# Four instead of three of eight K-tile pairs by seven products in the gate and up phases of a two-layer encoder trunk

## The chip, the core and the metric

One Trainium2 chip; the kernel runs on one of its cores. The metric is the device time of one execution in microseconds (us). TensorE (PE) does the matrix products, with its weight loads (PEld) beside them; VectorE (DVE) and ScalarE (ACT) do the elementwise work; GpSimd (POOL) does next to nothing here; SyncE (SP) issues the loads of weights.

## What is computed

Two layers over x (256 rows, 2048 columns, float32): layer 0 is an attention and convolution mixer, layer 1 a gMLP mixer with a layer norm, and each is followed by an RMSNorm and a SwiGLU block of hidden width 5632. The change lies in the SwiGLU blocks above all:

```
def swiglu(h, w_gate, w_up, w_down):
    return (jax.nn.silu(h @ w_gate) * (h @ w_up)) @ w_down

for layer in range(2):
    h = rms_norm(x, mix_norm[layer])
    x = x + (mixer_ab(h, ...) if layer == 0 else mixer_c(h, ...))
    h = rms_norm(x, ffn_norm[layer])
    x = x + swiglu(h, w_gate[layer], w_up[layer], w_down[layer])
return rms_norm(x, final_norm)
```

## The kernel before

**Precision.** Every large product is float32 by three matmuls (`three`, L439): each operand is split into a high part in fp32r (a cast on ACT) and a low part (source minus high part, a subtraction on DVE), and high x high, high x low and low x high are added up in PSUM. For weights the tiles are `raw` (as loaded), `whi` and `wlo`.

**Phases and steps.** The phases are ab_in, ab_out, up0, down0, c_in, c_out, up1, down1. A phase is cut into blocks of 512 output columns, a block into steps. A step takes 4 tiles of weights of 128x512: in an ordinary phase four K-tiles; in up0 and up1 a pair of K-tiles of the gate and the same pair of the up matrix. `whi` and `wlo` have two buffers each and `raw` has three, so the parts of step t+1 are made while PE works on step t, into the buffers that step t-1 has left.

**Up phases** (`run_mixed`, L501). Eleven blocks of eight steps, steps 0 to 7 of a block here. A step is a 2x2x2 product of blocks (two row halves, two K-tiles, gate and up), done in one of two ways, as the string `MIX` says: kind N by eight products, kind S by seven (Strassen's way). Each product is three matmuls of 128x512, so an N step has 24 and an S step 21. All products of a block go into seven accumulators q1 to q7, one PSUM bank each (`BANKS`, L490); the bank left over takes transposes. N uses the raw weight tiles. S needs sums of them in `tt` (`combine_first` L203, one subtraction of 128x1024; `combine_rest` L212, two of 128x512), `whi` and `wlo` of `tt`, and for three products also high and low parts `ha`, `la` of three raw tiles (`prep_a` L196, 128x1536). `tt`, `ha` and `la` have one buffer each. The activations come in matching sums, their parts are `fh` and `fl` (`x_forms`, L377).

**End of a block** (`ends`, L830). Seven additions on DVE with one ACT copy turn the accumulators into gate `sg` and up `hh` (`first`, `sums_a`, `sums_b`), ACT applies Silu (`gate`), DVE multiplies (`product`, two instructions). `h_transposes` (L819) then turns `hh` by two groups of four transposes on PE, each followed by an ACT copy to `h`. In an up phase both groups use the one spare bank, so the second group waits for the first copy, and the second copy for the second group.

**Order.** ACT and DVE run what the code emits in the order in which it emits it (`manual_schedule`), in the up phases throughout; PE's order is set by a scheduler when the program is built. At the end of step t the code emits the preparation of step t+2 (`prep`, L220): in an up phase both casts, then the jobs listed for `before[t+1]`, then the low part in two instructions of 128x1024. `end_step` does the same in the ordinary phases. Jobs put off by `later` are emitted at their due half step (`jobs_due`).

Of the kernel before, what the change touches and what calls it, by code (L numbers as in the profile page):

```python
# [16 lines left out]
P = 128  # L17
S = 256
# [28 lines left out]

MIX = "NNSNSNSN"  # L50

# [9 lines left out]
def trunk_kernel(  # L61
# [134 lines left out]
    def prep_a(t):  # L196

        hi = mixw[0].tile([P, 3, NB], F32R, tag="ha", name="ha")
        lo = mixw[0].tile([P, 3, NB], F32R, tag="la", name="la")
        split(hi, lo, raws[t][:, 1:4, :])  # L200
        parts_a[t] = (hi, lo)

    def combine_first(t):  # L203

        load(t)
# [6 lines left out]
    def combine_rest(t):  # L212

        r, tt = raws[t], sums[t]
# [5 lines left out]
    def prep(t, between=()):  # L220

        if t >= len(steps) or t in parts:
            return
        load(t)
        s = steps[t]
        r = sums.pop(t) if s.kind == "S" else raws[t]
        hi = wpool.tile([P, RC, NB], F32R, tag="whi", name="whi", bufs=W_BUFS)
        lo = wpool.tile([P, RC, NB], F32R, tag="wlo", name="wlo", bufs=W_BUFS)
        halves = [slice(0, 2), slice(2, 4)]
        if s.kind == "std":  # L230
            for fn in between:
                fn()
            for h in halves:
                split(hi[:, h, :], lo[:, h, :], r[:, h, :])
        else:
            for h in halves:
                nc.scalar.copy(hi[:, h, :], r[:, h, :])  # L237
            for fn in between:
                fn()
            for h in halves:  # L240
                nc.vector.tensor_tensor(  # L241
                    out=lo[:, h, :], in0=r[:, h, :], in1=hi[:, h, :].bitcast(F32),
                    op=ALU.subtract,
                )
        parts[t] = (hi, lo)
        if s.pi in operand:
            operand[s.pi].split(s.k0 // RC)

    sums = {}
    operand = {}  # L250

# [249 lines left out]
    def run_mixed(pi, lhs, ends):  # L501

        mixed[0] = True
        order = ExitStack()
        order.enter_context(  # L510
            tc.manual_schedule(engines={mybir.EngineType.Activation, mybir.EngineType.DVE})
        )
# [5 lines left out]
        last_s = MIX.rindex("S")  # L518
        ps, seen, left = {}, set(), {}
        before = {t: [] for t in range(lo_t, hi_t + 3)}  # L520
        after = {t: [] for t in range(lo_t - 1, hi_t + 3)}
        for t in range(lo_t, hi_t):
            i = (t - lo_t) % n
            if steps[t].kind != "S":
                continue
            early = i == MIX.index("S") and t - 3 >= lo_t
            (after[t - 3] if early else before[t - 2]).append(lambda t=t: combine_first(t))
            after[t - 2].append(lambda t=t: combine_rest(t))
            after[t - 1].append(lambda t=t: prep_a(t))
        for t in range(lo_t + n - 1, hi_t, n):  # L530
            first, sums_a, sums_b, gate, product = ends(steps[t].key, ps)
            after[t - n + 1 + last_s].append(first)
            after[t].insert(0, sums_a)
            before[t + 1][0:0] = [sums_b, gate]
            before[t + 2].insert(0, product)
        for fn in before[lo_t]:
            fn()
        for t in range(lo_t, hi_t):
# [9 lines left out]
            prods = LAST_S if i == last_s else PRODUCTS[s.kind]  # L548
            for j, (q, fa, group, slot) in enumerate(prods):
# [10 lines left out]
            for fn in after[t]:  # L560
                fn()
            parts_a.pop(t, None)
            del parts[t]
            cur[0] += 1
            load(t + LOAD_AHEAD)
            if t + 1 < hi_t:
                prep(t + PREP_AHEAD, before[t + 1])
            else:
                order.close()
                prep(t + PREP_AHEAD)  # L570
                for fn in before[t + 1] + before[t + 2]:
                    fn()
        mixed[0] = False

    cur = [0]
# [238 lines left out]
    def ffn(pi, st, nst):  # L814
# [14 lines left out]

        def ends(j, ps):  # L830


            def first():
                g = fpool.tile([P, M, NB], F32, tag="sg", name="sg")
                h = fpool.tile([P, M, NB], F32, tag="hh", name="hh")
                left[j], right[j] = g, h
# [4 lines left out]
            def sums_a():  # L841
                g, h = left[j], right[j]
                add(h[:, 0, :], ps[2], h[:, 0, :])
                add(g[:, 0, :], ps[5], g[:, 0, :])
                add(g[:, 1, :], ps[5], h[:, 1, :])

            def sums_b():
                g, h = left[j], right[j]
                add(g[:, 0, :], ps[3], g[:, 0, :])
                add(h[:, 1, :], ps[4], h[:, 1, :])  # L850

            def gate():
                g = left[j]
                for m in reversed(range(M)):
                    nc.scalar.activation(
                        g[:, m, :], g[:, m, :], AF.Silu, scale=st.r[:, m : m + 1]
                    )

            def product():
                g, h = left.pop(j), right.pop(j)  # L860
# [7 lines left out]
            return first, sums_a, sums_b, gate, product  # L868

        run_mixed(pi, st, ends)  # L870
        close_pool("forms", "mixw")
        xpool[0] = open_pool("x_next", "left")
        hT.split_pool = open_pool("split", "left")
        operand[pi + 1] = hT
        for n in range(PREP_AHEAD):
            hT.split(n)
# [41 lines left out]
    def layer_norm():  # L918
# [20 lines left out]
        for n in range(4):  # L939
            sl = slice(n * NB, (n + 1) * NB)  # L940

            def block(sl=sl):
                for m in range(M):
                    a = vt[:, m, sl]
                    nc.vector.tensor_scalar(  # L945
                        out=a, in0=a, scalar1=mu[:, m : m + 1], scalar2=rs[:, m : m + 1],
                        op0=ALU.add, op1=ALU.mult,
                    )
                    nc.vector.tensor_tensor(out=a, in0=a, in1=lng[:, sl], op=ALU.mult)  # L949
                    nc.vector.tensor_tensor(out=a, in0=a, in1=lnb[:, sl], op=ALU.add)  # L950
# [156 lines left out]
```

## Time and profile before

| | |
|---|---|
| time, median of three runs | 2119.1 us (2117.6 to 2122.2) |
| the profiled execution: its time / its span | 2118.6 us / 2116.7 us |
| busy: PE, DVE, ACT | 99%, 71%, 53% of the span |
| granted PE clock, mean | 0.994 of full speed |
| up0 | from 390.3 to 861.9 us of the span |
| up1 | the same length, from 1390 us on |

Views used: the page's totals and its chain of waits; windows, which give the busy time of each engine in a stretch; and timelines of one engine, in which a row is a run of like instructions with its start, its length, and in brackets the idle time before it and what ended that. DVE and ACT begin an instruction before the one in front of it has ended, so what an instruction costs its engine is the distance from start to start. The same holds for PE.

### The profile page before, as it was taken

How to read it: one execution, taken by the hardware profiler on the slowest of the kernel's cores; microseconds unless marked ns; L12 is line 12 of the kernel's file. 1: busy time of each engine (PE TensorE's matmuls, PEld its weight loads, DVE VectorE, ACT ScalarE, POOL GpSimd, SP SyncE). 2: the span in 40 equal slices, each digit the busy share in tenths (PEclk: the TensorE clock that was granted, in tenths of full speed). 3: DMA queues.
4: the chain of work that ended last, by engine and by line, in shares of the span. 5: the costliest groups of instructions: out<-in, count | busy, mean ns of one | idle time of the engine just before them, and what ended most of it. 6: DMA issues, size and time to landing. Idle time of an engine off the chain costs nothing.

```text
span 2116.7 us, 24028 instructions
## 1 busy us (share of the span) xinstructions
PE 2086.0 (99%) x9356; PEld 1722.0 (81%) x9356; DVE 1504.7 (71%) x1597; ACT 1115.7 (53%) x1318; POOL 17.8 (1%) x37
## 2 busy tenths in 40 slices
PE   8999999999999999999999999999999999999998
PEld 6888888788888888788888878878888888878886
DVE  4545556788888888667664465578888888866675
ACT  5444445555555555555555534555555555555554
POOL 1000000000000000000000000000000000000000
PEclk9999999999999999999999999999999999999999
DMA  6555555465556555655555554546555655555554
GB/s 243 182 173 174 185 184 194 160 206 192 201 196 203 195 200 194 232 186 191 195 191 189 181 173 169 195 160 213 184 199 199 209 189 199 200 198 193 188 196 139
DMA packets 205345, 404.80 MB, mean 191 GB/s; under 512 B 9420, under 2 KB 10032, under 8 KB 204976
## 3 DMA queue, kind: packets, MB, share of 16 engines
q1 hardware_dynamic: 203296, 397.45, 55.4%
q0 software_dynamic: 1328, 4.77, 0.7%
q8 instruction: 73, 1.20, 0.2%
q10 hardware_dynamic: 608, 1.06, 0.1%
q14 instruction: 40, 0.33, 0.0%
HBM read 401.14 MB, written 2.10 MB: 191 GB/s over the span
## 4 chain that ended last, share of the span: by engine, by line
PE 95%; DVE 1%; DMA 1%; ACT 1%; issue 1%; SPq 0%; POOLq 0%; POOL 0%; ACTq 0%; DVEq 0%
PE b L440 31%; PE b L442 31%; PE b L441 31%; PE b L346 2%; DMA raw<-in_ab_w_in_dram 1%; DVE wlo L194 1%; ACT whi L193 0%; PE b L382 0%; PE b L961 0%; PE b L653 0%; ACT junk L929 0%; DVE vt L949 0%; DVE vt L945 0%; PE b L697 0%; ACT ha L193 0%
## 5 line engine op out<-in xcount | busy, mean ns | idle before, releaser
L194 DVE TENSOR_TENSOR wlo<-raw,whi 128x1024 fp32r<-128x1024 f32 x400 | 471.7, 1219 | 244.4 <-ACT whi L193 244.3
L193 ACT CAST whi<-raw 128x1024 fp32r<-128x1024 f32 x400 | 400.0, 1049 | 257.8 <-PE b L442 217.4
L441 PE MATMUL b<-wlo,fh 128*128 128x512 f32 x1144 | 448.9, 393 | 0.0
L442 PE MATMUL b<-whi,fl 128*128 128x512 f32 x1144 | 445.1, 389 | 0.0
L440 PE MATMUL b<-whi,fh 128*128 128x512 f32 x1144 | 381.1, 392 | 0.0
L237 ACT CAST whi<-raw 128x1024 fp32r<-128x1024 f32 x220 | 220.3, 1050 | 177.0 <-PE b L442 93.4
L241 DVE TENSOR_TENSOR wlo<-raw,whi 128x1024 fp32r<-128x1024 f32 x220 | 258.9, 1218 | 34.3 <-ACT whi L237 34.3
L441 PE MATMUL b<-wlo,jh 128*128 128x512 f32 x704 | 275.4, 391 | 0.4 <-DVE wlo L194 0.4
L442 PE MATMUL b<-whi,jl 128*128 128x512 f32 x704 | 274.6, 390 | 0.7 <-DVE jl L194 0.7
L440 PE MATMUL b<-whi,jh 128*128 128x512 f32 x704 | 250.4, 392 | 6.1 <-ACT jh L193 6.1
L441 PE MATMUL b<-wlo,xh 128*128 128x512 f32 x640 | 253.1, 396 | 1.9 <-DVE wlo L194 1.9
L442 PE MATMUL b<-whi,xl 128*128 128x512 f32 x640 | 251.6, 394 | 0.3 <-DVE xl L371 0.3
L440 PEld LDWEIGHTS b<-whi,fh 128*128 128x128 f32 x1144 | 213.6, 188 | 45.6 <-ACT whi L237 0.6
L442 PEld LDWEIGHTS b<-whi,fl 128*128 128x128 f32 x1144 | 215.0, 188 | 43.4
L441 PEld LDWEIGHTS b<-wlo,fh 128*128 128x128 f32 x1144 | 214.8, 188 | 43.3
L440 PE MATMUL b<-whi,xh 128*128 128x512 f32 x640 | 243.5, 399 | 2.6 <-ACT xh L367 2.6
L194 DVE TENSOR_TENSOR jl<-h,jh 128x1024 fp32r<-128x1024 f32 x88 | 107.6, 1224 | 152.9 <-ACT jh L193 152.9
L237 ACT CAST whi<-tt 128x1024 fp32r<-128x1024 f32 x132 | 134.7, 1053 | 128.7 <-PE b L442 90.3
L193 ACT CAST jh<-h 128x1024 fp32r<-128x1024 f32 x88 | 92.6, 1054 | 204.4 <-PE b L441 204.4
L241 DVE TENSOR_TENSOR wlo<-tt,whi 128x1024 fp32r<-128x1024 f32 x132 | 157.2, 1220 | 58.0 <-ACT whi L237 58.0
L440 PEld LDWEIGHTS b<-whi,jh 128*128 128x128 f32 x704 | 132.5, 189 | 34.0 <-ACT jh L193 6.9
L442 PEld LDWEIGHTS b<-whi,jl 128*128 128x128 f32 x704 | 132.7, 189 | 29.8 <-DVE jl L194 2.2
(148 smaller groups left out, 2308.3 us busy)
## 6 DMA issues: line engine op xcount, KB each, us to landing
raw<-in_ffn_w_gate_dram SPq DMA_DIRECT2D x176, 512.0 KB, 3.6
raw<-in_ffn_w_up_dram SPq DMA_DIRECT2D x176, 512.0 KB, 4.5
raw<-in_ffn_w_down_dram SPq DMA_DIRECT2D x88, 1024.0 KB, 4.9
raw<-in_ab_w_in_dram SPq DMA_DIRECT2D x47, 1024.0 KB, 5.0
raw<-in_c_w_in_dram SPq DMA_DIRECT2D x32, 1024.0 KB, 5.1
raw<-in_ab_w_out_dram SPq DMA_DIRECT2D x16, 1024.0 KB, 4.9
raw<-in_c_w_out_dram SPq DMA_DIRECT2D x16, 1024.0 KB, 4.9
x<-in_x_dram SPq DMA_DIRECT2D x3, 512.0 KB, 12.2
```

What stands on the lines that cost most here:

```text
L193: nc.scalar.copy(hi, src)
L194: nc.vector.tensor_tensor(out=lo, in0=src, in1=hi.bitcast(F32), op=ALU.subtract)
L237: nc.scalar.copy(hi[:, h, :], r[:, h, :])
L241: nc.vector.tensor_tensor(out=lo[:, h, :], in0=r[:, h, :], in1=hi[:, h, :].bitcast(F32), op=ALU.subtract,)
L346: nc.tensor.transpose(out=pt[:, j * S + m * P : j * S + (m + 1) * P], in_=src[:, m, c0 + j * P : c0 + (j + 1) * P], identity=ident,)
L440: nc.tensor.matmul(ps, lhsT=ah, rhs=bh, start=start, stop=False)
L441: nc.tensor.matmul(ps, lhsT=ah, rhs=bl, start=False, stop=False)
L442: nc.tensor.matmul(ps, lhsT=al, rhs=bh, start=False, stop=stop)
```

## The change

`MIX` becomes SNSNSNSN: in each block step 0 turns from N to S, so four steps of eight are by seven products. The lists `before` and `after` give way to a table `WINDOWS` with one line for each step t of a block. Words before the colon are emitted ahead of the matmuls of step t, words behind it after them; +1 or +2 names the step that a word works for, and without it that is t+1:

- c0, c1: casts of the first and second half (128x1024) of `whi`
- s: the low part `wlo` in one instruction of 128x2048; s0, s1: its halves, used for step 1 alone
- t1, t2: `combine_first` and `combine_rest`; ha, la: the two halves of `prep_a`
- first, end_a1, end_a2, end_b, gate, product: the end of a block, in smaller pieces

The first S step of a block is now its first step, and q5 is the first accumulator that it lists. `LAST_S`, another order of the products in the last S step, is gone. Where phases meet: step 0 and 1 of an up phase are prepared by `prep` while ab_out or c_out still runs, and the fixed order of ACT and DVE begins at step 2; at the end of an up phase `handover` opens the pools and splits the first `h` tile ahead of the last sums. At the program's start the transposes of x's third and fourth quarter are due one half step earlier, and the layer norm's work is queued in eight jobs instead of four.

```diff
-MIX = "NNSNSNSN"
+MIX = "SNSNSNSN"
+WINDOWS = (
+    "c0 c1 end_b gate la+0 : s0 s1 t1+2",
+    "c0 t2+1 c1 s : ha+1 la+1",
...
+    def low_part(t, h):
+        hi, lo = parts[t]
+        r = sums[t] if steps[t].kind == "S" else raws[t]
+        sl = HALF[h]
+        nc.vector.tensor_tensor(
+            out=lo[:, sl, :], in0=r[:, sl, :], in1=hi[:, sl, :].bitcast(F32), op=ALU.subtract
+        )
+    HALF = {"0": slice(0, 2), "1": slice(2, 4), "": slice(0, 4)}
...
-    LAST_S = tuple(sorted(PRODUCTS["S"], key=lambda q: (1, 6, 7, 2, 5, 3, 4).index(q[0])))
...
+            if t == lo_t + 2:
+                order.enter_context(
+                    tc.manual_schedule(
+                        engines={mybir.EngineType.Activation, mybir.EngineType.DVE}
+                    )
+                )
...
+            pre, _, post = WINDOWS[i].partition(":")
+            window(t, pre)
             jobs_due(2 * t)
...
+            window(t, post)
             parts_a.pop(t, None)
             del parts[t]
             cur[0] += 1
             load(t + LOAD_AHEAD)
-            if t + 1 < hi_t:
-                prep(t + PREP_AHEAD, before[t + 1])
+            if t + 2 == hi_t:
+                prep(t + 2)
+        order.close()
+        handover()
+        prep(hi_t + 1)
+        for op in ("end_b", "gate", "product"):
+            block_end[0].pop(op)()
...
-        later(2 * n - 2, lambda n=n: x_transposes(st, n))
+        later(2 * n - 3, lambda n=n: x_transposes(st, n))
```

In the following listings of the program's order, equal instructions that follow each other are one row. First DVE, from the product of one block to the sums of the next. Before:

```order
L862 SCALAR_TENSOR_TENSOR hh_3454<-hh_3454,rstd_2849,sg_3453 128x512 x2
L241 TENSOR_TENSOR wlo_3543<-tt_3494,whi_3542 128x1024 x2
L194 TENSOR_TENSOR la_3575<-raw_3458,ha_3574 128x1536
L208 TENSOR_TENSOR tt_3585<-raw_3539 128x1024
L241 TENSOR_TENSOR wlo_3582<-raw_3496,whi_3581 128x1024 x2
L216 TENSOR_TENSOR tt_3585<-raw_3539,tt_3585 128x512 x2
L241 TENSOR_TENSOR wlo_3632<-tt_3585,whi_3631 128x1024 x2
```

Now:

```order
L896 SCALAR_TENSOR_TENSOR hh_3456<-hh_3456,rstd_2860,sg_3455 128x512 x2
L264 TENSOR_TENSOR wlo_3655<-raw_3582,whi_3654 128x2048
L235 TENSOR_TENSOR tt_3682<-raw_3613 128x1024
L247 TENSOR_TENSOR tt_3682<-raw_3613,tt_3682 128x512 x2
L264 TENSOR_TENSOR wlo_3688<-tt_3682,whi_3687 128x2048
L223 TENSOR_TENSOR la_3733<-raw_3613,ha_3731 128x1536
L235 TENSOR_TENSOR tt_3742<-raw_3684 128x1024
L264 TENSOR_TENSOR wlo_3739<-raw_3651,whi_3738 128x2048
```

The product stands in step 4 now, and the low part of an S step is one instruction behind the two that make the second half of its source. The first and third row of the low parts belong to steps 5 and 7, the one between to step 6.

Then ACT, where the two copies to `h` stand (b_3604 and b_3610, b_3707 and b_3713 are the spare bank at each of its two uses). Before:

```order
L237 CAST whi<-raw 128x1024 x2
L823 COPY h_3603<-b_3604 128x512
L823 COPY h_3603<-b_3610 128x512
L237 CAST whi<-tt 128x1024 x2
L193 CAST ha<-raw 128x1536
```

Now:

```order
L258 CAST whi<-tt 128x1024 x2
L859 COPY h_3706<-b_3707 128x512
L859 COPY h_3706<-b_3713 128x512
L216 CAST ha<-raw 128x1536
L258 CAST whi<-raw 128x1024 x2
```

The copies stood ahead of the casts of an S step (step 4); now they stand behind the casts of step 6 and ahead of its `ha`.

Last PE, around the second group of transposes. Before:

```order
L440 MATMUL b0_3509<-whi_3581,fh3_2580 128x512
L440 MATMUL b2_3523<-whi_3581,fh3_2580 128x512
L346 MATMUL b4_3610<-ident_84,hh_3454 128x128 x4
L441 MATMUL b0_3509<-wlo_3582,fh3_2580 128x512
L442 MATMUL b0_3509<-whi_3581,fl3_2581 128x512
```

Now:

```order
L479 MATMUL b1_3512<-whi_3687,fh6_2928 128x512
L479 MATMUL b5_3516<-whi_3687,fh6_2928 128x512
L479 MATMUL b7_3520<-whi_3687,fh6_2928 128x512
L479 MATMUL b3_3524<-whi_3687,fh6_2928 128x512
L385 MATMUL b4_3713<-ident_84,hh_3456 128x128 x4
L480 MATMUL b1_3512<-wlo_3688,fh6_2928 128x512
```

The group stood among the first matmuls of step 3 (fh3), an N step; it stands now behind the first four of step 6 (fh6), an S step, in every block that has it. The first group stands ahead of the first matmul of step 5 that uses `wlo`, with 20 matmuls of step 5 between that point and step 6.

## Rows read from the trace of the kernel before

**Rows 1.** The page, part 1: busy us, share, instructions of each engine.

```profile
PE 2086.0 (99%) x9356; PEld 1722.0 (81%) x9356; DVE 1504.7 (71%) x1597; ACT 1115.7 (53%) x1318; POOL 17.8 (1%) x37
```

**Rows 2.** The page, part 4: the chain that ended last, shares by engine.

```profile
PE 95%; DVE 1%; DMA 1%; ACT 1%; issue 1%; SPq 0%; POOLq 0%; POOL 0%; ACTq 0%; DVEq 0%
```

**Rows 3.** Windows, one up0 block: length; busy PE, PEld, DVE, ACT, POOL; PEclk; DMA.

```profile
479.96:522.42 42.46, 42.46 (x192) 35.09 (x192) 36.65 (x38) 22.94 (x24) 0.00 (x0) 1.00 0.58 198
```

**Rows 4.** Timeline of DVE, same block: start us, length, instruction [idle before <-releaser].

```profile
485.03 1.41 DVE L216 TENSOR_TENSOR tt<-raw,tt 128x512 f32<-128x512 f32 x2
486.36 1.41 DVE L862 SCALAR_TENSOR_TENSOR hh<-hh,rstd,sg 128x512 f32<-128x512 f32 x2
487.68 2.35 DVE L241 TENSOR_TENSOR wlo<-tt,whi 128x1024 fp32r<-128x1024 f32 x2
489.95 1.75 DVE L194 TENSOR_TENSOR la<-raw,ha 128x1536 fp32r<-128x1536 f32 x1
491.62 1.22 DVE L208 TENSOR_TENSOR tt<-raw 128x1024 f32<-128x1024 f32 x1
492.75 2.36 DVE L241 TENSOR_TENSOR wlo<-raw,whi 128x1024 fp32r<-128x1024 f32 x2
...
499.03 2.36 DVE L241 TENSOR_TENSOR wlo<-tt,whi 128x1024 fp32r<-128x1024 f32 x2 [2.59 <-ACT whi L237]
...
507.76 2.43 DVE L241 TENSOR_TENSOR wlo<-tt,whi 128x1024 fp32r<-128x1024 f32 x2
...
521.70 0.68 DVE L828 TENSOR_TENSOR sg<-b,sg 128x512 f32<-128x512 f32 x1
522.29 0.68 DVE L828 TENSOR_TENSOR sg<-b,hh 128x512 f32<-128x512 f32 x1
```

**Rows 5.** Timeline of ACT, same block.

```profile
497.46 0.59 ACT L823 COPY h<-b 128x512 f32<-128x512 f32 x1 [4.07 <-PE b L346]
497.94 2.00 ACT L237 CAST whi<-tt 128x1024 fp32r<-128x1024 f32 x2
...
507.88 1.06 ACT L237 CAST whi<-tt 128x1024 fp32r<-128x1024 f32 x1 [1.33 <-DVE tt L216]
508.84 1.48 ACT L193 CAST ha<-raw 128x1536 fp32r<-128x1536 f32 x1
```

**Rows 6.** Timeline of PE, same block.

```profile
482.51 0.84 PE L440 MATMUL b<-whi,fh 128*128 128x512 f32 x3
483.19 0.39 PE L441 MATMUL b<-wlo,fh 128*128 128x512 f32 x1
...
496.83 0.60 PE L346 MATMUL b<-ident,hh 128*128 128x128 f32 x4
```

**Rows 7.** Timeline of PE, the third step of up0.

```profile
404.64 0.40 PE L442 MATMUL b<-whi,fl 128*128 128x512 f32 x1
407.73 1.39 PE L440 MATMUL b<-ha,fh 128*128 128x512 f32 x3 [2.69 <-ACT ha L193]
...
411.94 0.85 PE L440 MATMUL b<-whi,fh 128*128 128x512 f32 x3
```

**Rows 8.** Timeline of PE where down0 begins.

```profile
861.70 0.39 PE L442 MATMUL b<-whi,fl 128*128 128x512 f32 x1
865.12 0.54 PE L440 MATMUL b<-whi,jh 128*128 128x512 f32 x1 [3.03 <-ACT jh L193]
...
869.27 0.40 PE L440 MATMUL b<-whi,jh 128*128 128x512 f32 x1
```

**Rows 9.** Timeline of PE in c_in, beside the layer norm.

```profile
1223.46 0.50 PE L441 MATMUL b<-wlo,xh 128*128 128x512 f32 x1 [1.89 <-DVE wlo L194]
```

**Rows 10.** Windows, the four us after that wait.

```profile
1224.00:1228.00 4.00, 4.00 (x12) 3.13 (x12) 4.00 (x7) 0.17 (x1) 0.00 (x0) 0.59 0.59 169
```

**Rows 11.** Timeline of PE at the program's start.

```profile
24.98 0.50 PE L440 MATMUL b<-whi,xh 128*128 128x512 f32 x1 [2.26 <-ACT xh L367]
```

**Rows 12.** Timeline of ACT at the program's start.

```profile
22.56 1.99 ACT L193 CAST whi<-raw 128x1024 fp32r<-128x1024 f32 x2 [5.78 <-DMA raw<-in_ab_w_in_dram]
```

More of the change, by code (lines that the diff above doesn't have):

```diff
@@ L46 @@
 PREP_AHEAD = 2
-MIX = "NNSNSNSN"
+MIX = "SNSNSNSN"
+WINDOWS = (
+    "c0 c1 end_b gate la+0 : s0 s1 t1+2",
+    "c0 t2+1 c1 s : ha+1 la+1",
+    "c0 c1 s : t1+2",
+    "c0 t2+1 c1 s : ha+1 la+1",
+    "c0 c1 product s : t1+2",
+    "c0 t2+1 c1 s : ha+1 la+1",
+    "c0 c1 t1+2 s : t2+2 first",
+    "c0 c1 ha+1 : end_a1 s end_a2",
+)
 S_FORMS, N_FORMS = 7, 6
@@ L218, in combine_rest, with cast_half, prep @@
             )
-    def prep(t, between=()):
+    def cast_half(t, h):
+        if t not in parts:
+            load(t)
+            hi = wpool.tile([P, RC, NB], F32R, tag="whi", name="whi", bufs=W_BUFS)
+            lo = wpool.tile([P, RC, NB], F32R, tag="wlo", name="wlo", bufs=W_BUFS)
+            parts[t] = (hi, lo)
+        r = sums[t] if steps[t].kind == "S" else raws[t]
+        nc.scalar.copy(parts[t][0][:, HALF[h], :], r[:, HALF[h], :])
+    def low_part(t, h):
+        hi, lo = parts[t]
+        r = sums[t] if steps[t].kind == "S" else raws[t]
+        sl = HALF[h]
+        nc.vector.tensor_tensor(
+            out=lo[:, sl, :], in0=r[:, sl, :], in1=hi[:, sl, :].bitcast(F32), op=ALU.subtract
+        )
+    def prep(t):
         if t >= len(steps) or t in parts:
@@ L224, in prep @@
         load(t)
[L225 to L247, printed above, removed]
+        if steps[t].kind == "S":
+            combine_first(t)
+            combine_rest(t)
+        for h in "01":
+            cast_half(t, h)
+            low_part(t, h)
+        if steps[t].kind == "S":
+            prep_a_hi(t)
+            prep_a_lo(t)
+        if steps[t].pi in operand:
+            operand[steps[t].pi].split(steps[t].k0 // RC)
+    HALF = {"0": slice(0, 2), "1": slice(2, 4), "": slice(0, 4)}
+    whole = set()
+    sums = {}
     sums = {}
@@ L497, in trunk_kernel, with run_mixed @@
     }
-    LAST_S = tuple(sorted(PRODUCTS["S"], key=lambda q: (1, 6, 7, 2, 5, 3, 4).index(q[0])))
-    def run_mixed(pi, lhs, ends):
+    def run_mixed(pi, lhs, ends, handover):
         mixed[0] = True
         order = ExitStack()
-        order.enter_context(
-            tc.manual_schedule(engines={mybir.EngineType.Activation, mybir.EngineType.DVE})
-        )
         lo_t = cur[0]
@@ L517, in run_mixed, with window @@
         n = len(MIX)
-        last_s = MIX.rindex("S")
         ps, seen, left = {}, set(), {}
-        before = {t: [] for t in range(lo_t, hi_t + 3)}
-        after = {t: [] for t in range(lo_t - 1, hi_t + 3)}
-        for t in range(lo_t, hi_t):
[L523 to L538, printed above, removed]
+        block_end = [None]
+        def window(t, text):
+            for word in text.split():
+                op, _, dt = word.partition("+")
+                tt = t + int(dt or 1)
+                if op in ("c0", "c1", "s0", "s1", "s"):
+                    if tt < hi_t and tt not in done:
+                        (cast_half if op[0] == "c" else low_part)(tt, op[1:])
+                elif dt:
+                    if tt < hi_t:
+                        assert steps[tt].kind == "S"
+                        {"t1": combine_first, "t2": combine_rest, "ha": prep_a_hi,
+                         "la": prep_a_lo}[op](tt)
+                elif block_end[0] and op in block_end[0]:
+                    block_end[0].pop(op)()
+        done = set(parts)
+        for t in range(lo_t, hi_t):
+            if t == lo_t + 2:
+                order.enter_context(
+                    tc.manual_schedule(
+                        engines={mybir.EngineType.Activation, mybir.EngineType.DVE}
+                    )
+                )
             s = steps[t]
             i = s.k0 // 2
+            pre, _, post = WINDOWS[i].partition(":")
+            window(t, pre)
             jobs_due(2 * t)
@@ L559, in run_mixed @@
             now[0] = 2 * t + 2
-            for fn in after[t]:
-                fn()
+            if i == MIX.rindex("S"):
+                block_end[0] = ends(s.key, ps)
+            window(t, post)
             parts_a.pop(t, None)
@@ L866, in product, with handover @@
                 later(3, lambda: h_transposes(j, h))
[L868 to L876, printed above, removed]
+            return dict(first=first, end_a1=end_a1, end_a2=end_a2, end_b=end_b, gate=gate,
+                        product=product)
+        def handover():
+            close_pool("forms", "mixw")
+            xpool[0] = open_pool("x_next", "left")
+            hT.split_pool = open_pool("split", "left")
+            operand[pi + 1] = hT
+            hT.split(0)
+        run_mixed(pi, st, ends, handover)
         if nst:
```

65 lines of the change are left out of this document (35 added, 30 removed).

## The prediction

> **What bounds the kernel now.** I read the totals first: PE is busy 99% of the span, DVE 71%, ACT 53% [rows 1]. The chain of waits says the same, with 95% of the path on PE [rows 2]. Then one stage by itself, since the change lies in the up phases: a block of up0 takes 42.46 us, PE is busy in all of it at full clock, and DVE is busy 36.65 of it [rows 3]. So a matmul less is time gained there, but only as long as DVE, whose share is 86% in this stage and not 71%, keeps up. From here on I work with distances from start to start. A matmul of 128x512 takes (483.19 - 482.51) / 3 = 0.227 us [rows 6]. With 183 matmuls a block is 183 x 0.2267 = 41.49, so the eight transposes cost 0.97.
>
> **The change: what PE saves.** One N step of each block becomes S: 24 - 21 = 3 matmuls, 22 blocks, 66 x 0.2267 = 15.0 us. A block of PE's work becomes 180 x 0.2267 + 0.97 = 41.78.
>
> **What DVE gets.** Durations from [rows 4]: t2 (two of 512) 486.36 - 485.03 = 1.33; product (two) 1.32; low part in two halves 489.95 - 487.68 = 2.27; la 1.67; t1 492.75 - 491.62 = 1.13; a sum of 512 from PSUM 0.60 (521.70 to 522.29). A low part of 128x2048 is in no row. From above it is bounded by the two halves, 2.27; from 1024 (1.135) to 1536 (1.67) the slope is 0.535 for 512 elements, so 1.67 + 0.535 = 2.20, which I take, as 1536 is the nearest row; a slope through zero from the same row gives 1.67 x 4/3 = 2.23, and four slopes with no fixed part 2.14, the lower bound.
> - Before: 8 x 2.27 + 3 x (1.67 + 1.13 + 1.33) + 7 x 0.60 + 1.32 = 36.07. DVE could stand 6.39 us in each block and PE did not notice.
> - After: 7 x 2.20 + 2.27 + 4 x (1.67 + 1.13 + 1.33) + 7 x 0.60 + 1.32 = 39.71. PE's block is 41.78, so DVE may now wait 2.07 us in a block. The question is how much it must wait.
>
> **Waits of DVE that the new order makes.** Both follow from the order in which instructions stand, and DVE and ACT have no other work to pull forward.
> - Steps 1, 3 and 5: t2, then the whole low part s of the S step. s needs the cast c1, and c1 needs t2. In the trace t2 makes way at 507.76, the cast runs from 507.88 to 508.94 [rows 5], and a low part that needs it can start 0.03 later, at 508.97: 1.21 us after DVE was free. Today the first half of the low part runs in that gap, which is why the pair at 507.76 is only 2.43 long [rows 4]. As one instruction it waits: 3 x 1.21 = 3.63 in a block.
> - Step 6: la stands on DVE behind s, and needs ha, which on ACT stands behind the second copy to h, which needs the second group of transposes, which on PE stands behind all of step 5 and four matmuls of step 6. Count from the end of s of step 5: 0.11 until PE sees it, 20 matmuls 4.53, four more 0.91, the transposes 0.60 [rows 6], copy 0.48 (497.46 to 497.94), ha 1.48 [rows 5], and twice 0.03 between engines: 8.17. In that time DVE has t1 1.13, t2 1.33, the wait 1.21 and s 2.20: 5.87. It waits 2.30. The same chain can be seen today: ACT stood 4.07 at the second copy [rows 5], and DVE 2.59 behind it [rows 4]; with 6.39 to spare this cost nothing.
>
> I followed the other waits round the block with these durations (casts behind PE's release of a buffer, the end sums behind the last product of q2 to q5, q5's bank behind end_a2 at the next block's ninth matmul, la of step 0 behind end_b, the loads into raw behind its last reader): none of them ends later than DVE's own work. So DVE's period is 39.71 + 3.63 + 2.30 = **45.64 us a block**, against 42.46 now: 3.18 more. PE, which needs 41.78, stands 3.9 us in each block: some 1.5 before the low part of step 7 (behind la, t1 and s: 8.64 after the start of step 6, when PE is there at 7.1), 0.8 before la of step 0, 0.3 to 0.4 at each of ha, la and casts of step 6, the rest in pieces under 0.2.
>
> **Where phases meet.**
> - Start of an up phase. PE stands 2.69 for the first ha, and then runs at a lower clock: from 404.87 to 411.94 it does 11 matmuls, 2.49 us of work in 7.07, a loss of 4.58 [rows 7]. Now steps 0 and 1, with their S parts, are made while ab_out's last steps run. Followed through, every part is there before PE; the first wait is 0.35 in step 7. Block 0 has no sums, product or copies of a block before it, so DVE is not late in it. Its end comes 4.58 + 0.68 - 0.35 = 4.9 earlier. The ten distances to the following blocks cost 3.18 each: +31.8.
> - End of an up phase. Today 861.93 to 869.27 holds nine matmuls: a loss of 5.30 [rows 8]. Now jh stands on ACT ahead of the second step's casts. Count from the end of the last s of step 7: PE ends at 0.11 + 4.53 = 4.64; DVE has first 1.20, the low part of down0's step 0 2.27, five sums 3.00, jl 1.13, done at 7.60. PE goes on at 7.71 with the fifth matmul, 2.16 behind. Gain 3.1; at worst, with the clock as low as today, 1.4.
> - Program start. PE waits 2.26 for xh [rows 11], as xh stood on ACT behind a cast that waited for its load until 22.56 [rows 12]. Ahead of that cast it is done in time; but PE then waits for the cast, 23.6 instead of 24.98, and the next load holds it later. I take 1.0; bounds 0 and 2.3.
> - Layer norm. DVE's order comes out the same as before, so the wait of 1.89 there [rows 9] stays: 0.
>
> **Sum.** Per up phase -4.9 + 31.8 - 3.1 = +23.8, twice +47.6, start -1.0: +46.6. Against the profiled execution's own 2118.6 (which is the median less 0.5): **2165 us**, 2.2% slower.
>
> **A rule against a row.** The rows say that a low part in one instruction saves 2.27 - 2.20 = 0.07 and, behind t2, costs 1.21. The Trainium skill, Perfetto Trace Analysis, section Optimizing Scalar/DVE Operations, has it both ways: grouping into larger operations can raise throughput if the engine is saturated, and breaking up instructions may let work finish sooner if an engine that isn't saturated makes others stand. By its first sentence alone DVE would be charged its 39.71 and no wait, and the time would be the first rival's, 2087; the bracket at 499.03 [rows 4], a wait and not work, speaks for the second.
>
> **Rivals.**
> - *DVE's waits fit into its 2.07 us, and PE stays the bound* (faster). It decides where DVE's waits in a block stay under 2.07, which needs two of the three casts behind t2 and the wait for ha to vanish. Then 2118.6 - 15.0 - 2 x 4.6 - 2 x 3.1 - 1.0 = 2087. For it: PE had no wait in any steady block, with DVE idle 2.59 at one place. Against it: that place comes back, and the row of casts is fixed.
> - *Only the wait for ha vanishes*, say because PE reaches the transposes earlier than I count: 39.71 + 3.63 = 43.34, 0.88 a block more than now. 20 x 0.88 - 2 x 4.9 - 2 x 3.1 - 1.0 = +0.6: 2119, no change.
> - *The clock falls with PE's stalls* (slower still). In c_in PE stood 1.89 and the four us behind it were granted 0.59 [rows 9, 10]; the largest new stall is 1.5, with nearly 1 more in the four us ahead of it, and no row has such a stall, so this is open. A fall costs 4.58 - 2.86 = 1.7 at the start of up0, where PE stood from 404.87 to 407.73 [rows 7]. Behind the stall in step 7 PE stands again for 1.0 in step 0, which hides part of it: 0.3 to 1.7 a block, 20 blocks, 6 to 34: 2171 to 2199.
> - *The change doesn't do what it says* holds for the layer norm, whose order is the same; that is in the sum.
>
> **How the numbers follow.** Forecast 0.70, by itself 2152 to 2180 (the low part's 2.14 to 2.27 is +-0.5 a block, 10 us in all; the edges of phases +-4); a falling clock 0.12; no change 0.09; PE still the bound 0.09. A measurement of this kernel can tell about 0.2%, 4.2 us, from no change. Faster by that: 0.09 + 0.02 = 0.11; within it 0.04; slower 0.70 + 0.12 + 0.03 = 0.85. The range has to leave out 0.2: the first rival, most of the second, and the tail of the third, so 2128 to 2198.
>
> **What would show it.** In the changed profile: blocks of up0 start 45.6 apart; DVE is busy some 88% of a block and waits 1.2 at L264 for whi, three times, and 2.3 at L223 for ha, once; PE waits at its matmuls for la (L223) and wlo (L264), 3.9 in all; the waits at the starts of up0 and up1 are gone, that of down0 falls to about 2, that in c_in stays. I am wrong if PE runs through a block without a wait, or if DVE's low part behind t2 starts at once; half wrong if the second copy on ACT isn't waited for.

## The result, and the profile after

The changed kernel takes **2175.4 us** (median of four runs, 2174.8 to 2180.8) against 2119.3 for the kernel before on the same chip (2117.6 to 2122.2): a ratio of **1.0269**, 95% interval 1.0249 to 1.0289. The forecast was 2165, 2.2% slower. The direction held and the waits stood where the prediction put them; the loss came out 10 us larger.

The page of the changed kernel, part 1 (busy us, share, instructions) and part 4 (the chain that ended last):

```profile
PE 2112.3 (97%) x9290; PEld 1691.7 (78%) x9290; DVE 1585.2 (73%) x1539; ACT 1150.1 (53%) x1340; POOL 17.8 (1%) x37
...
PE 70%; DVE 20%; issue 5%; ACT 3%; DMA 1%; DVEq 0%; SPq 0%; ACTq 0%; POOLq 0%; POOL 0%
```

PE has its 66 matmuls less (9356 to 9290), and yet its busy time went up: the record of a matmul reaches past the start of the next (0.39 long, 0.227 apart) and is 0.50 long behind a stop (612.57 below), so that part of each stop counts as busy. The second row is the telling one: in [rows 2] PE held 95% of the path; now a fifth of it runs over DVE.

A block of up0 after the change, from la of step 6 to the next la of step 6, in the view of windows (length; busy PE, PEld, DVE, ACT, POOL; granted clock; DMA share; GB/s):

```profile
561.20:607.42 46.22, 44.22 (x188) 33.87 (x188) 40.30 (x34) 24.53 (x26) 0.00 (x0) 1.00 0.53 183
```

It answers to [rows 3]: 46.22 and not 42.46, at full clock. The end of that block on DVE, with the brackets that the prediction named:

```profile
596.84 2.28 DVE L264 TENSOR_TENSOR wlo<-raw,whi 128x2048 fp32r<-128x2048 f32 x1
599.04 1.21 DVE L235 TENSOR_TENSOR tt<-raw 128x1024 f32<-128x1024 f32 x1
600.29 1.42 DVE L247 TENSOR_TENSOR tt<-raw,tt 128x512 f32<-128x512 f32 x2
602.82 2.29 DVE L264 TENSOR_TENSOR wlo<-tt,whi 128x2048 fp32r<-128x2048 f32 x1 [1.11 <-ACT whi L258]
607.42 1.76 DVE L223 TENSOR_TENSOR la<-raw,ha 128x1536 fp32r<-128x1536 f32 x1 [2.31 <-ACT ha L216]
609.10 1.22 DVE L235 TENSOR_TENSOR tt<-raw 128x1024 f32<-128x1024 f32 x1
610.24 2.28 DVE L264 TENSOR_TENSOR wlo<-raw,whi 128x2048 fp32r<-128x2048 f32 x1
```

ACT in the same place:

```profile
602.70 0.58 ACT L859 COPY h<-b 128x512 f32<-128x512 f32 x1
605.43 0.59 ACT L859 COPY h<-b 128x512 f32<-128x512 f32 x1 [2.15 <-PE b L385]
605.91 1.48 ACT L216 CAST ha<-raw 128x1536 fp32r<-128x1536 f32 x1
```

And PE, from the first matmul that needs the low part of step 5 to the first that needs that of step 7:

```profile
599.18 0.50 PE L480 MATMUL b<-wlo,fh 128*128 128x512 f32 x1
...
604.80 0.60 PE L385 MATMUL b<-ident,hh 128*128 128x128 f32 x4
...
610.72 0.61 PE L479 MATMUL b<-whi,fh 128*128 128x512 f32 x2
612.57 0.50 PE L480 MATMUL b<-wlo,fh 128*128 128x512 f32 x1 [1.24 <-DVE wlo L264]
```

Read together: the low part behind t2 stands 1.11 for its second cast, three times a block (the ones at 581.78 and 591.64 have the same bracket as that at 602.82). la of step 6 stands 2.31 for ha; ha is behind the second copy on ACT; the copy is behind PE's second transposes. PE then stops at the low part of step 7.

### The profile page after: what moved, and what is told of

Same layout as the page of the kernel before. It is cut to its first block, busy times and chain, and to the rows that moved or that the text cites. A ratio compares the mean times of both kernels' runs of the same rounds, so it can differ in the third digit from the quotient of the medians.

```text
span 2172.8 us, 23983 instructions
## 1 busy us (share of the span) xinstructions
PE 2112.3 (97%) x9290; PEld 1691.7 (78%) x9290; DVE 1585.2 (73%) x1539; ACT 1150.1 (53%) x1340; POOL 17.8 (1%) x37
## 4 chain that ended last, share of the span: by engine, by line
PE 70%; DVE 20%; issue 5%; ACT 3%; DMA 1%; DVEq 0%; SPq 0%; ACTq 0%; POOLq 0%; POOL 0%
PE b L480 23%; PE b L481 22%; PE b L479 22%; DVE wlo L264 9%; DVE la L223 3%; DVE tt L247 2%; DVE tt L235 2%; ACT whi L258 2%; DVE sg L864 1%; DVE hh L864 1%; PE b L385 1%; ACT ha L216 1%; DMA raw<-in_ab_w_in_dram 1%; DVE hh L896 1%; PE b L997 0%
## 5 line engine op out<-in xcount | busy, mean ns | idle before, releaser
L264 DVE TENSOR_TENSOR wlo<-raw,whi 128x1024 fp32r<-128x1024 f32 (+1 forms) x508 | 671.9, 1357 | 239.9 <-ACT whi L258 239.4
L258 ACT CAST whi<-raw 128x1024 fp32r<-128x1024 f32 x574 | 573.9, 1049 | 285.4 <-PE b L481 224.1
L480 PE MATMUL b<-wlo,fh 128*128 128x512 f32 x1056 | 421.1, 399 | 24.1 <-DVE wlo L264 23.5
L481 PE MATMUL b<-whi,fl 128*128 128x512 f32 x1056 | 412.6, 391 | 0.0
L258 ACT CAST whi<-tt 128x1024 fp32r<-128x1024 f32 x176 | 184.8, 1052 | 364.1 <-DVE tt L235 295.5
L479 PE MATMUL b<-whi,fh 128*128 128x512 f32 x1056 | 355.8, 395 | 0.0
L264 DVE TENSOR_TENSOR wlo<-tt,whi 128x2048 fp32r<-128x2048 f32 (+1 forms) x90 | 201.6, 2242 | 73.5 <-ACT whi L258 73.3
L479 PEld LDWEIGHTS b<-whi,fh 128*128 128x128 f32 x1056 | 196.7, 188 | 59.5 <-ACT whi L258 8.3
L223 DVE TENSOR_TENSOR la<-raw,ha 128x1536 fp32r<-128x1536 f32 x88 | 154.1, 1752 | 46.9 <-ACT ha L216 46.9
L480 PEld LDWEIGHTS b<-wlo,jh 128*128 128x128 f32 x704 | 132.2, 188 | 28.1 <-DVE wlo L264 0.8
```

The costliest lines, as they stand in the source:

```text
L223: nc.vector.tensor_tensor(out=lo, in0=raws[t][:, 1:4, :], in1=hi.bitcast(F32), op=ALU.subtract)
L258: nc.scalar.copy(parts[t][0][:, HALF[h], :], r[:, HALF[h], :])
L264: nc.vector.tensor_tensor(out=lo[:, sl, :], in0=r[:, sl, :], in1=hi[:, sl, :].bitcast(F32), op=ALU.subtract)
L479: nc.tensor.matmul(ps, lhsT=ah, rhs=bh, start=start, stop=False)
L480: nc.tensor.matmul(ps, lhsT=ah, rhs=bl, start=False, stop=False)
L481: nc.tensor.matmul(ps, lhsT=al, rhs=bh, start=False, stop=stop)
```

## The experiments

All are the changed kernel with an edit, except the one that says otherwise. The last column is the distance from block to block in up0.

| kernel | median us | ratio to before, 95% interval | block |
|---|---|---|---|
| changed | 2175.4 | 1.0269 (1.0249 to 1.0289) | 46.22 |
| e1: halves behind t2, three places | 2178.6 | 1.0276 (1.0259 to 1.0293) | 46.47 |
| e2: ha ahead of the copies | 2148.0 | 1.0131 (1.0116 to 1.0146) | 44.60 |
| e3: both | 2173.1 | 1.0249 (1.0234 to 1.0264) | 46.24, 45.81 in turn |
| e4: halves, late second copy | 2094.2 | 0.9876 (0.9861 to 0.9891) | 42.10 |
| e5: kernel before, whole low parts | 2119.1 | 0.9998 (0.9988 to 1.0007) | 42.48 |
| e6: three S steps, new edges | 2101.4 | 0.9917 (0.9902 to 0.9932) | 42.45 |
| e7: halves at two places | 2163.3 | 1.0210 (1.0195 to 1.0225) | 45.57 |
| e8: late second copy, whole parts | 2128.5 | 1.0048 (1.0031 to 1.0065) | 43.84 |
| e9: e4, la of step 0 earlier | 2092.6 | 0.9877 (0.9863 to 0.9892) | 42.10 |
| e11: e4, ha ahead of the copies | 2090.0 | 0.9858 (0.9841 to 0.9874) | 41.86 |
| e12: e11, la of step 0 earlier | 2087.2 | 0.9847 (0.9832 to 0.9861) | 41.81 |

### Taking the two waits away, one at a time: e1, e2, e3

e1, in WINDOWS of steps 1, 3 and 5:

```diff
-    "c0 t2+1 c1 s : ha+1 la+1",
+    "c0 t2+1 c1 s0 s1 : ha+1 la+1",
```

> The changed kernel, with the low parts that stand behind t2 (of steps 2, 4 and 6, made while steps 1, 3 and 5 run) in two halves again; everything else stays. Theory (DVE's waits set the period of a block, not DVE's work): the first half fills the wait for the cast c1, so that a part costs about 2.4 from the end of t2 and not 1.1 + 2.2 = 3.3, 0.9 less, in steps 2 and 4; that of step 6 is hidden, since la behind it still waits for ha. Block 46.2 - 1.8 = 44.4 us, time 2175 - 20 x 1.8 = about 2139. Rival one (DVE's work of four S steps is too much in any order): halves are 3 x 0.07 more work a block, 2175 to 2180. Rival two (only the wait for ha counts): 2175.

Measured: 2178.6, a block of 46.47. **The expectation failed**, by 39 us, though the waits for c1 are gone. DVE and PE where the block ends:

```profile
599.49 2.42 DVE L264 TENSOR_TENSOR wlo<-tt,whi 128x1024 fp32r<-128x1024 f32 x2
606.93 1.76 DVE L223 TENSOR_TENSOR la<-raw,ha 128x1536 fp32r<-128x1536 f32 x1 [5.01 <-ACT ha L216]
```

```profile
602.49 1.07 PE L479 MATMUL b<-whi,fh 128*128 128x512 f32 x4
603.39 0.39 PE L480 MATMUL b<-wlo,fh 128*128 128x512 f32 x1
...
604.30 0.60 PE L385 MATMUL b<-ident,hh 128*128 128x128 f32 x4
...
606.95 0.96 PE L479 MATMUL b<-ha,fh 128*128 128x512 f32 x3 [1.11 <-ACT ha L216]
```

What DVE saved turned into a wait of 5.01 for ha in place of 2.31. And the second group of transposes stands behind eight matmuls of step 6 (602.49 to 604.30), not behind four as at 604.80 in the changed kernel. Only ACT's and DVE's orders are written out by hand. PE's comes from the scheduler, and it moved with the edit. Each matmul ahead of the transposes delays copy, ha, la and the low part of step 7.

e2 moves ha of step 6 ahead of the copies on ACT:

```diff
-    "c0 t2+1 c1 s : ha+1 la+1",
+    "c0 t2+1 c1 ha+1 s : la+1",
```

> The changed kernel, with one word moved: ha of step 6 stands on ACT ahead of the two copies to h and not behind them. The low parts behind t2 stay whole. Theory: la of step 6 no longer waits for ha (2.3 us a block); the casts of step 7 still stand behind the copies and give back 0.1 to 0.2. Block 46.2 - 2.2 = 44.0, time 2175 - 20 x 2.2 = about 2131. Rival one (DVE's work is too much in any order): 2175. Rival two (only the wait for c1 counts): 2175, with the 2.3 turning up at the next low part.

Measured: 2148.0, a block of 44.60. The expectation missed by 17 us, 12 of them in the blocks (44.60, not 44.0); the other 5 were not traced. The wait for ha is gone; the casts of step 7, behind the second copy, give back 0.67 and not 0.1 to 0.2:

```profile
601.02 1.75 DVE L223 TENSOR_TENSOR la<-raw,ha 128x1536 fp32r<-128x1536 f32 x1
602.68 1.22 DVE L235 TENSOR_TENSOR tt<-raw 128x1024 f32<-128x1024 f32 x1
604.57 2.29 DVE L264 TENSOR_TENSOR wlo<-raw,whi 128x2048 fp32r<-128x2048 f32 x1 [0.67 <-ACT whi L258]
```

46.22 - 2.31 + 0.67 = 44.58: DVE's own sum closes. So the wait for ha is worth its length, less what comes back at the casts. On PE the transposes stand behind seven matmuls here, three more than in the changed kernel; that delays the second copy, and 3 x 0.227 = 0.68 would be enough to explain why more came back than expected.

e3 has both edits.

> Both edits: low parts behind t2 in halves, and ha of step 6 ahead of the copies. Theory: the two gains add and the half hidden before in step 6 comes free (3 x 0.9 + 2.3 = 5.0), but then the casts of step 7, behind the second copy on ACT, are late by about 1.0. Block 46.2 - 5.0 + 1.0 = 42.2, near PE's own 41.8; time 2175 - 20 x 4.0 = about 2095, below the kernel before. Rival one (DVE's work is too much in any order): 2170 or more. A rival in between (DVE's 40.3 us of work leave PE bubbles at every hand-over even without these waits): 43 to 43.5 a block, 2110 to 2120.

Measured: 2173.1. It failed by 78 us, for the reason of e1 in a stronger form: the scheduler put the transposes behind fifteen matmuls of step 6, so that the second copy and the casts behind it came so late that the low part of step 7 stood 4.07. PE's clock also fell in every second block (last section), but that is the smaller part: the blocks without a fall are still 45.81 long.

```profile
556.43 1.22 DVE L235 TENSOR_TENSOR tt<-raw 128x1024 f32<-128x1024 f32 x1
561.72 2.29 DVE L264 TENSOR_TENSOR wlo<-raw,whi 128x2048 fp32r<-128x2048 f32 x1 [4.07 <-ACT whi L258]
```

After these three the theory had to be widened: **two loops** set the block, and they are nearly equally long. One is DVE's, its work and its waits. The other runs through PE: second transposes, copy, ha, then DVE's work from la of step 6 by t1 and the low part of step 7 up to la of step 0, and from there PE's matmuls round to the next second transposes. In the changed kernel the first part of it, from the transposes to the matmul with the low part of step 7, takes 612.57 - 604.80 = 7.77, and PE has only the transposes and 21 matmuls, some 5.1 us, to do in that time.

### Taking the loop through PE away: e4 and e8

e4 has the halves of e1, and the second half of the transposes with its copy is released half a step later, so that on ACT it comes behind ha of step 6 and the casts of step 7:

```diff
-                later(3, lambda: h_transposes(j, h))
+                later(3, lambda: h_transposes(j, h, 0))
+                later(4, lambda: h_transposes(j, h, 1))
```

> Both edits, and the second half of the transposes of h with its copy half a step later, so that neither ha of step 6 nor the casts of step 7 stand behind that copy on ACT. Theory: DVE's period would be 41.2 and PE's is 41.8, so PE is the bound again: blocks 41.8 to 42.0, time 2087 to 2092. If the casts of step 7 aren't what is late in the kernel with both edits, it is the same as that one. Rival one (DVE's work is too much in any order): 2170 or more.

The text speaks of both edits; the kernel that ran has the halves and the late copy, and ha at its old place in WINDOWS (with ha moved too it is e11). Measured: 2094.2, 1.2% faster than the kernel before and 2 us above the range expected, a block of 42.10:

```profile
591.49:633.59 42.10, 42.06 (x190) 34.48 (x189) 40.75 (x37) 24.64 (x25) 0.00 (x0) 1.00 0.60 200
```

The rival that DVE's work of four S steps is too much in any order is out: DVE does 40.75 in a block of 42.10. What held e3 back was the place of the second transposes and their copy: e11 (below) is e3 with the late copy, and its blocks are 41.86.

e8 has the late copy alone, with the low parts whole, and so measures the waits for c1 where the other loop is gone.

> The changed kernel with the second half of the transposes of h and its copy half a step later, and the low parts behind t2 left whole. Theory: the loop through PE is gone and DVE's wait for ha with it, so DVE's loop is its work and the three waits for c1: 46.2 - 2.3 = 43.9, time 2175 - 46 = about 2129; against 42.1 of the same kernel with halves, the whole parts then cost 1.8 a block. Rival (the c1 waits cost nothing, only the copy did): 2094, as with halves.

Measured: 2128.5, a block of 43.84; DVE's waits of 1.11 are the only ones left on it:

```profile
592.58 1.42 DVE L247 TENSOR_TENSOR tt<-raw,tt 128x512 f32<-128x512 f32 x2
595.12 2.29 DVE L264 TENSOR_TENSOR wlo<-tt,whi 128x2048 fp32r<-128x2048 f32 x1 [1.11 <-ACT whi L258]
597.32 1.75 DVE L223 TENSOR_TENSOR la<-raw,ha 128x1536 fp32r<-128x1536 f32 x1
```

Whole parts cost 43.84 - 42.10 = 1.74 a block, 34 us in all, once nothing else holds the block.

### The two loops told apart: e7

e1 and the changed kernel differ in DVE's order and, unmeant, in PE's. With halves in steps 2 and 4 only, the transposes stand behind four matmuls again (602.19):

```diff
 # WINDOWS of steps 1 and 3 only; step 5 keeps "s"
-    "c0 t2+1 c1 s : ha+1 la+1",
+    "c0 t2+1 c1 s0 s1 : ha+1 la+1",
```

> The changed kernel, with halves behind t2 in steps 2 and 4 only; step 6's part stays whole. In the first experiment PE's own order moved too: the second transposes of h stood behind eight matmuls of step 6 there, behind four in the changed kernel; here they stand behind four again. Theory as it now stands: two loops set the block. DVE's is 46.2 and falls by 2 x 0.9 to 44.4. The other runs through PE (second transposes, copy, ha, la, t1, low part of step 7, and PE back round to the transposes); the first experiment shows it at 46.47 with the transposes four matmuls later, so 46.47 - 4 x 0.227 = 45.56 here. Block 45.6, time 2175 - 20 x 0.66 = about 2162. Theory as first told (DVE's waits alone): 44.4, 2139. Rival (DVE's work alone sets it): 2175.

Measured: 2163.3, a block of 45.57; expected with two loops 45.56 and 2162:

```profile
559.25:604.82 45.57, 43.55 (x188) 34.01 (x188) 40.69 (x36) 24.53 (x26) 0.00 (x0) 1.00 0.56 185
```

The loop can be followed in e7: PE's only stops between one second transposes (602.19) and the next (647.73) are in step 6 and 7 and, the last of them, at la of step 0:

```profile
619.48 0.50 PE L480 MATMUL b<-la,fh 128*128 128x512 f32 x1 [0.47 <-DVE la L223]
```

Up to there it is 17.29, by ACT and DVE; from there PE has 122 matmuls and the first transposes to do, about 28.3, and does not stop. In the changed kernel the second transposes have the same place, so there DVE's loop is 46.22 and the loop through PE can be taken as 45.57. Without two of DVE's waits for c1, 1.8 us, only 0.65 a block was to be had. The distance to e1, 46.47 - 45.57 = 0.90, is the four more matmuls that stand ahead of the transposes there, 4 x 0.227 = 0.91.

### The edges of the phases alone: e6

e6 keeps the changed kernel's work at the phase edges, with three S steps, halves and the late copy:

```diff
-MIX = "SNSNSNSN"
+MIX = "NNSNSNSN"
-    "c0 c1 end_b gate la+0 : s0 s1 t1+2",
-    "c0 t2+1 c1 s : ha+1 la+1",
-    "c0 c1 s : t1+2",
+    "c0 c1 end_b gate : s0 s1 t1+2",
+    "c0 t2+1 c1 s0 s1 : ha+1 la+1",
+    "c0 c1 product s : t1+2",
...
-    "c0 c1 t1+2 s : t2+2 first",
-    "c0 c1 ha+1 : end_a1 s end_a2",
+    "c0 c1 s : first",
+    "c0 c1 : end_a1 s end_a2",
```

> The changed kernel's order of work at the phase edges and at the program's start, with three S steps in a block again as before (steps 2, 4 and 6), low parts behind t2 in halves and the late second copy, so that PE should be the bound inside the blocks, as before: 42.46 a block. What is left against the kernel before is the edges alone. The prediction's own numbers: 2 x 4.9 at the starts of the up phases, 2 x 3.1 at their ends, 1.0 at the program's start: 2119 - 17 = about 2102; 2098 to 2106. If the edges bring nothing: 2119. If a wait inside the blocks is left, the blocks are longer than 42.5 and the time says little of the edges.

Measured: 2101.4 with blocks of 42.45, as before. The edges are a gain by themselves, close to the 17 us that the prediction had; what else lies in that number is said below.

### A whole low part where there is slack: e5

e5 is the kernel before, with one edit:

```diff
-            for h in halves:
-                nc.vector.tensor_tensor(
-                    out=lo[:, h, :], in0=r[:, h, :], in1=hi[:, h, :].bitcast(F32),
-                    op=ALU.subtract,
-                )
+            nc.vector.tensor_tensor(out=lo, in0=r, in1=hi.bitcast(F32), op=ALU.subtract)
```

> The kernel before with one edit: in the gate and up phases each low part of a weight tile is one instruction of 128x2048 and not two of 128x1024, with the order as it was; where it stands behind t2 it waits for the second cast. Theory (a wait of DVE costs only where DVE's loop is as long as PE's): three waits of about 0.9 more a block eat into DVE's 6.4 us of slack, and PE sees nothing: 2119, within 4. Rival (an instruction of 128x2048 behind a cast costs PE by itself, since PE needs the first half sooner than the second): some 0.9 a time, three to eight times a block, 20 blocks: 2170 or more.

Measured: 2119.1, ratio 0.9998 (0.9988 to 1.0007). DVE stands for the casts five times in a block, 5.9 us in all, and PE not once:

```profile
585.47 2.29 DVE L240 TENSOR_TENSOR wlo<-tt,whi 128x2048 fp32r<-128x2048 f32 x1 [3.15 <-ACT whi L237]
...
595.21 2.29 DVE L240 TENSOR_TENSOR wlo<-tt,whi 128x2048 fp32r<-128x2048 f32 x1 [1.12 <-ACT whi L237]
...
600.05 2.29 DVE L240 TENSOR_TENSOR wlo<-raw,whi 128x2048 fp32r<-128x2048 f32 x1 [0.87 <-ACT whi L237]
```

The same instruction costs nothing here, where one of its waits is 1.12 and another 3.15, and 34 us between e8 and e4, where it stands three times a block with a wait of 1.11. The wait has no price of its own; the loop that it lies in has.

### A version that beats both: e9, e11, e12

In e4's block DVE is nearly without a gap, and the longer of its two waits is 0.63, for ha of step 6 behind the first copy:

```profile
633.59 1.76 DVE L223 TENSOR_TENSOR la<-raw,ha 128x1536 fp32r<-128x1536 f32 x1 [0.63 <-ACT ha L216]
```

e9 is e4 with la of step 0 ahead of end_b:

```diff
-    "c0 c1 end_b gate la+0 : s0 s1 t1+2",
+    "c0 c1 la+0 end_b gate : s0 s1 t1+2",
```

> The fastest kernel so far (halves, late second copy), with la of step 0 ahead of the two sums end_b on DVE and not behind them. In that kernel PE's only stop in a block is at la of step 0, 0.2 to 0.3 us. Theory: it goes, block 42.1 to 41.8, time 2094 - 20 x 0.25 = about 2089. If the product, now 1.7 later, is late for the transposes, it gains nothing or loses up to 1.7 a block: 2094 to 2128.

Measured: 2092.6, a block of 42.10 as in e4. The 2089 expected did not come, and the block did not grow either, so the product was not late. The move alone brings nothing that can be told apart: DVE's loop was the bound.

e11 is e4 with ha of step 6 ahead of the first copy as well (the edit of e2), e12 has the edit of e9 on top.

> The kernel with halves and the late second copy, with ha of step 6 ahead of the first copy to h on ACT too. In the blocks of that kernel, 42.10 long, DVE works almost without a gap, 0.64 of it a wait for ha of step 6 behind the first copy; PE's own work is 41.8. Theory: DVE's loop falls to 41.5, PE's 41.8 is the bound by itself: 2094 - 20 x 0.3 = about 2088. Rival (42.1 is what PE itself needs): 2094.

> As the one before, with la of step 0 ahead of the sums end_b as well. Alone that edit brought nothing, DVE being the bound. Theory: with DVE's loop at 41.5, PE's stop at la of step 0 (0.3 us) is what is left, and it goes if la is earlier: 2086 to 2089. Rival (42.1 is what PE itself needs): 2092.

Measured: 2090.0 and 2087.2, blocks of 41.86 and 41.81. The block of e12, and its page:

```profile
546.26:588.07 41.81, 41.81 (x190) 34.49 (x189) 40.85 (x38) 24.65 (x26) 0.00 (x0) 1.00 0.61 201
```

```profile
PE 2063.0 (99%) x9290; PEld 1703.9 (82%) x9290; DVE 1596.4 (77%) x1605; ACT 1152.4 (55%) x1340; POOL 17.8 (1%) x37
```

PE is the bound again, at 41.81, where the prediction worked out 41.78 for PE's work. e12 is 1.5% faster than the kernel before (interval 1.4 to 1.7%), and 88 us faster than the changed kernel with the same arithmetic.

## Why the prediction was right, and where it fell short

**What PE saves: right.** 66 matmuls less; PE's own block is 41.81 in e12, against 41.78.

**The low part of 128x2048: right.** 599.04 - 596.84 = 2.20, the value taken from the slope.

**The waits for c1: right in size.** From the start of t2 to the start of the low part it is 602.82 - 600.29 = 2.53, against 1.33 + 1.21 = 2.54, three times a block.

**The wait for ha: right in place, and close in size partly by luck.** The bracket of 2.31 counts from the end of the record before it; from start to start, as the prediction counts, the wait is 607.42 - 602.82 - 2.20 = 2.40 against 2.30. Two of its terms were short, the chain by 0.21 and DVE's t1 by 0.12 (both below), and they partly cancel here.

**DVE's period: mis-sized, and this is where the 10 us are.** 45.64 was predicted, 46.22 measured. Three terms were too small, taken from rows in which another instruction follows:
- t1 was charged 1.13, as in [rows 4], where a low part of other data follows. With t2 of the same tile right behind it, 1.25 (599.04 to 600.29). Twice a block outside the chain of ha: 0.24.
- The chain from the low part of step 5 to la of step 6 took 607.42 - 596.84 - 2.20 = 8.38 and not 8.17. From 599.18 to 604.80 PE needed 5.62 for what was charged 5.44 (4.53 + 0.91), of which 0.11 is that the first matmul there, behind the first transposes, takes 0.34 and not 0.227: 0.21 with the hand-overs.
- The first of the end sums, whose result the next one reads, took 0.72 and not 0.60: 0.12. The prediction took a later pair; the trace of the kernel before has 0.73 in the place in question:

```profile
516.72 0.69 DVE L828 TENSOR_TENSOR sg<-b,hh 128x512 f32<-128x512 f32 x1 [0.76 <-ACT hh L837]
517.45 0.69 DVE L828 TENSOR_TENSOR hh<-b,sg 128x512 f32<-128x512 f32 x1
```

Together 0.57 of the 0.58 that were missing; over 20 distances 11.6 us. That is more than the total missed, since the rest came out some 2 us better, most of it the clock in c_in (below). PE's stops lie where the prediction put them. From start to start they are 612.57 - 610.72 - 2 x 0.227 = 1.40 before the low part of step 7 (1.5 predicted; the bracket has 1.24), 0.65 before la of step 0 (0.8), 0.32 before ha of step 6 (0.3 to 0.4).

**Where phases meet: right.** The starts of up0 and up1 have no wait; the first is in step 7, as predicted (0.35, measured 0.44), and the end of up0 has 1.21 and 0.40 in place of the 3.03 of [rows 8]. The wait of 1.21, for a cast, is not in the prediction's count; that for jl, which is, ends last:

```profile
427.75 0.50 PE L480 MATMUL b<-wlo,fh 128*128 128x512 f32 x1 [0.44 <-DVE wlo L264]
...
893.40 0.39 PE L481 MATMUL b<-whi,fl 128*128 128x512 f32 x1
895.00 0.47 PE L479 MATMUL b<-whi,jh 128*128 128x512 f32 x1 [1.21 <-ACT whi L258]
...
896.64 0.50 PE L481 MATMUL b<-whi,jl 128*128 128x512 f32 x1 [0.40 <-DVE jl L209]
...
897.90 0.39 PE L479 MATMUL b<-whi,jh 128*128 128x512 f32 x1
```

From 893.63, the end of up0's last matmul, to 897.90 there are nine matmuls, 2.04: a loss of 2.23 against 2.16 predicted and 5.30 before. e6 has 17.4 us for the edges and the prediction 17.0, but they are not the same sum. Of the 17.0, 2 x (0.68 - 0.35) = 0.66 comes from step 0 as an S step and from the stop in step 7, and e6 has neither. In e6 the clock in c_in also stayed full, as in the next paragraph, and that is some 1.5 of the 17.4. Like for like it is about 15.9 against 16.3. The start of the program gave about 0.45 and not 1.0, inside its bounds; PE waits later instead, 1.93 at 32.07 for a cast whose weights came late.

**The layer norm: right that its wait stays, with one part not foreseen.** PE stands 1.89 as in [rows 9], but the four us behind it were granted full clock, where [rows 10] has 0.59:

```profile
1252.08 0.50 PE L480 MATMUL b<-wlo,xh 128*128 128x512 f32 x1 [1.89 <-DVE wlo L264]
```

```profile
1252.00:1256.00 4.00, 3.92 (x17) 3.27 (x18) 4.00 (x7) 0.80 (x1) 0.00 (x0) 1.00 0.36 95
```

That is some 1.5 us, and the order of work in c_in does not decide it by itself. In e5, with c_in in the order of the kernel before, the four us behind the same stop were granted full clock too:

```profile
1226.00:1230.00 4.00, 4.00 (x18) 3.31 (x19) 4.00 (x7) 0.59 (x1) 0.00 (x0) 1.00 0.45 116
```

In e4, with c_in in the order of the changed kernel, they were granted 0.60 (1213.50 to 1217.50). So the full clock in the changed kernel's profiled execution is luck; at the clock of [rows 10] that execution would have been some 11 us above the forecast and not 10.

**The rivals.** *PE stays bound* would have been 2087; e12 reached just that, 2087.2, but only with four further edits of the order (halves, late copy, ha and la earlier). *Only the wait for ha vanishes* is what e8 runs: predicted 43.34 a block and 2119, measured 43.84 and 2128.5, too low by the same mis-sized DVE terms. *The clock falls with PE's stops* is wrong for the changed kernel: its blocks were granted 1.00, as in the row of the block shown with the result.

**What the prediction did not see** is the second loop. It treated the waits for c1 and for ha as two terms to be added, and for the sum that did no harm, since DVE's loop was the longer. As prices they don't stand: two of the three waits for c1 alone were worth 0.65 a block (e7), the wait for ha alone 2.4 (e8), all together 4.1 (e4). Its condition for the first rival, that two of the three casts and the wait for ha must go, was not enough either: e3 took all of them away, and stood at 2173 with the transposes late on PE.

**The rule.** The Trainium skill, Perfetto Trace Analysis, section Optimizing Scalar/DVE Operations, has grouping for a saturated engine and breaking up for one that isn't saturated but makes others stand. The runs bear out the second half where DVE's loop is the bound: e4 against e8, halves are 34 us faster although three of them are 0.45 more work a block (DVE is busy 40.75 in e4, 40.30 in the changed kernel). Where DVE has slack (e5) or another loop is as long (e7), hardly or not. The Trainium skill, VectorE: DVE Perf Modes, section Rules for kernel authors, says, of DVE operations in a chain, to minimise their number and not the semaphores. e8 has fewer operations than e4 and is slower: the larger operation had to wait for a cast on ACT, a case of which that row does not speak, and the wait was dearer than the operation saved.

## What to carry to other kernels

Work out the period of a steady block as the longest loop, not as one engine's work plus its waits: a wait in the trace is what is left over on an engine, and taking it away pays only down to the next loop (0.65 of the 1.8 us expected). When DVE's and ACT's orders are written by hand and PE's is left to a scheduler, compare PE's order too after every edit: four matmuls ahead of a transpose moved 0.9 us a block, and in e3, with eleven more, the whole gain was gone until the copy was moved too. Merge two instructions only where both inputs are there at the same time, or where the engine has slack for the wait.

## What the runs showed of the hardware that was not expected

- **The clock behind the same stop differs.** In e3 PE stood 2.08 at the low part of step 7 in every block. Four us behind it, in one block and in the next:

```profile
564.00:568.00 4.00, 3.94 (x11) 3.18 (x12) 3.86 (x7) 2.43 (x2) 0.00 (x0) 0.63 0.70 229
...
612.00:616.00 4.00, 4.00 (x19) 3.18 (x18) 3.90 (x5) 2.81 (x3) 0.00 (x0) 1.00 0.65 242
```

  It fell in every second block of up0. The distance from block to block was 46.24 where it fell and 45.81 where not, so a fall cost 0.43: the wait of 0.47 for la of step 0, which follows in the other blocks, hid part of it. Behind the stop of 1.89 to 1.91 in c_in the four us were granted 0.59 in the kernel before, 0.60 in e4 and 0.66 in e2, and 1.00 in the changed kernel, e5, e6 and e12. What decides it was not tried.
- **On DVE the successor counts.** t1 takes 1.13 from start to start when a low part of another tile follows, and 1.25 when t2, which reads what it wrote, does. The first of the end sums shows the same step: 0.72, where the next sum reads its result, against 0.60 for the others. That the reading is the cause was not tested by a run of its own.
